# A two-layer diffusion backbone on one core: the layer norms' sums get precedence in the planned order, and constants and conditioning are prepared behind the first gated mixer

## The chip, the cores and the metric

The kernel runs on one core of one Trainium2 chip. The core has a matrix engine (TensorE, PE in the profile), three engines for elementwise work (VectorE: DVE, ScalarE: ACT, GpSimd: POOL) and a queue for transfers (SyncE: SP); each works through its own list of instructions in a fixed order and waits for the others by semaphores. The metric is device time in microseconds (us) of one execution; less is better.

## The reference

One inference step of a backbone with two layers, on 640 tokens (512 latent and 128 context) of 1024 channels. Each layer modulates its input by the conditioning (adaLN), runs three mixers side by side, merges them under gates, and ends both halves in a layer norm:

```python
def trunk_layer(x, cvec, l, P, pos, ctx):
    mod = jax.nn.silu(cvec) @ P['ada_w'][l] + P['ada_b'][l]
    sh1, sc1, g1, sh2, sc2, g2 = jnp.split(mod, 6, axis=-1)
    mix, ctx_out = token_mixer(x * (1.0 + sc1) + sh1, l, P, pos, ctx)
    x = layer_norm(ALPHA * x + g1 * mix, P['ln_g'][l, 0], P['ln_b'][l, 0])
    ff = conv_ffn(x * (1.0 + sc2) + sh2, l, P)
    x = layer_norm(ALPHA * x + g2 * ff, P['ln_g'][l, 1], P['ln_b'][l, 1])
    return x, ctx_out
```

`token_mixer` holds mixer A (retention, which needs the decays `log_sigmoid(ret_decay)`), mixer B (gated linear attention, the "gated mixer") and mixer C (differential attention, the third mixer, which needs one number lambda and a scaled gain per layer). There are four layer norms in all: mixer norm and FFN norm of the first layer, and the same of the second, whose FFN norm is the end of the program. Everything is computed in float32.

## The kernel before

**Tiles.** Activations lie transposed, as eight row tiles of 128 channels by 640 tokens. A projection streams its weights in blocks of 128 x 1024: SP loads `w`, ACT copies it to `whi` (a rounded high part), DVE or POOL subtracts to get `wlo`, and PE makes three matmuls of each piece: high weights by high input (`hh`), high by low input (`hl`), low weights by `hh`. Tokens come in two halves: the first is columns 256 to 640, in profile rows a 128x384 piece on PE and pieces of 256 and 128 on DVE and ACT; the second is columns 0 to 256.

**What sets the order.** The program is not issued as it is written. `Program.add` records every operation with its engine (some may go to DVE or POOL: `ANY`), an estimated cost and what it depends on; `Program.place` then plans the lists of all engines at once: of the operations that are ready, each engine takes the one with the smallest key. The key is the operation's place in the written program plus its argument `late`; a negative `late` gives precedence. An operation may be taken ahead of its place only within a window of the matrix work. On ACT the planner also counts the loads of function tables. What comes out is issued in that order, and on the chip an engine whose next instruction waits lets nothing behind it pass.

**A layer norm.** The projection in front of it (`pout` after the mixers, `pdn` after the FFN) makes its eight output blocks for the first half of the tokens, then for the second. `residual` adds each to the stream `xa` (DVE) and sums the blocks into `acc`. For the first half, `norm` makes the mean by a matmul with a matrix of ones (`pm<-acc`), subtracts it from the eight blocks, squares them on ACT, adds the squares up in a chain, and makes the variance by a matmul (`pv<-sq`); ACT turns it into `rs` by Ln and Exp, each behind a load of its function table. For the second half, `Shift` subtracts an early mean `mu` from half of the sums, and lets PE sum the squares (`pm<-sq`) and the blocks (`pm<-xa`); its `norm` puts a correction on that: a second `mu`, which is the square of the rest of the mean, `rs<-pm,mu` on DVE, Ln, Exp, and a last subtraction `xa<-xa,pm` from each block. `to_h` makes the next projection's input of each block: `hf` (DVE), `hh` (ACT), `hl` (DVE). The next projection is `pfa`/`pfb` after a mixer norm, `pq`/`pk` of the second layer's gated mixer after the first FFN norm; the last norm writes the output. `rescale` (POOL) brings `xa` to the scale of the next residual while the projection runs.

**The start.** `ada_first` makes the first layer's modulation by matmuls `pada` from loads `wada`; then the first projection runs, with its first weights still on their way. `pvv` is the projection of the gated mixer's values. At the start the program as written also prepares, for both layers, the decays `lg` (a series of tiny operations on 128 x 12), the third mixer's `nlam` and `gc`, the gated mixer's `gb`, and the conditioning `sB` (times its sigmoid, four steps of 128 x 512), from which later modulations are dot products on DVE.

Line 535 is every matmul, 556 an ACT operation, 568 a tensor-tensor operation, 582 one with a scalar and a tensor; the names tell them apart. After the change these are 536, 557, 569 and 583.

Of the kernel before, what the change touches and what calls it, by code (L numbers as in the profile page):

```python
# [138 lines left out]
RES = (0, 0)  # L139
RESC = 2  # L140
# [345 lines left out]
def hybrid_kernel(ctx, tc, io):  # L486
# [94 lines left out]
    def stt(out, a, s, b, op0, op1, eng=DVE):  # L581
        prog.add(eng, lambda e: ENG[e].scalar_tensor_tensor(out=real(out), in0=real(a), scalar=real(s), in1=real(b),  # L582
                                                            op0=op0, op1=op1), [out], [a, s, b], vcost(out.n, nptr(s)),
                 port=two(a, b))
# [50 lines left out]
    dma(sms[0], io["sm"][0])  # L635
# [5 lines left out]
    dma(cst[:, 0:128], io["cst"][:, 0:128])  # L641
# [22 lines left out]
    def ada_first(i):  # L664

        l = 0
        ps = mslot("pada")
        for k in range(KD):
            w = row("wada")
            dma(w[:, 0:512], io["adaW"][i, k])  # L670
            r = 32 * (k % 4)
            mm(ps[r:r + 32, 0:512], sc32[:, k, :], w[:, 0:512], start=(k < 4), stop=(k >= 4), free=r > 0)
        ev = row("ev")
        act(ev[:, 0:512], ps[:, 0:512])

# [128 lines left out]
    def norm(u, acc, half):  # L804
# [7 lines left out]
        for k in range(8):  # L812
            yield
            tt(u[k][:, c], u[k][:, c], pm[:, pc], SUB)
            p, q = q, row("sq")
            act(q[:, c], u[k][:, c], AF.Square)
            if k:
                tt(q[:, c], q[:, c], p[:, c], ADD, ANY)
# [5 lines left out]
    class Shift:  # L824
# [11 lines left out]
        def square(self, k):  # L836
            q = row("sq")
            act(q[:, self.c], self.u[k][:, self.c], AF.Square)
            mm(self.part(512), C("o1024"), q[:, self.c], start=(k == SECOND[0]), stop=(k == SECOND[7]))
# [17 lines left out]
        def norm(self):  # L857
            u, c, rs, dd = self.u, self.c, row("rs"), self.m
            act(dd[:, c], self.part(0), AF.Square)
            tt(rs[:, c], self.part(512), dd[:, c], SUB)  # L860
# [533 lines left out]

    lgs, lams = [], []
    for l in range(L):
        src = sms[l][:, SM["lgp"][0]:SM["lgp"][0] + 12]
        e = tiny([128, 12], "e")
        act(e, src, AF.Abs)
        act(e, e, AF.Exp, scale=-1.0)  # L1400
        den = tiny([128, 12], "den")
        ts(den, e, 2.0, ADD)
        recip(den, den)
        z = tiny([128, 12], "z")
        tt(z, e, den, MUL)
        z2 = tiny([128, 12], "z2")
        tt(z2, z, z, MUL)
        s = tiny([128, 12], "s")
        memset(s, 2.0 / 15, DVE)
        for n in (13, 11, 9, 7, 5, 3, 1):  # L1410
            tt(s, s, z2, MUL)
            ts(s, s, 2.0 / n, ADD)
        tt(s, s, z, MUL)
        lg = ctile([128, 12], f"lg{l}")
        ts(lg, src, 0.0, ALU.min)
        tt(lg, lg, s, SUB)
        nlg = ctile([128, 12], f"nlg{l}")
        ts(nlg, lg, -1.0, MUL)
        lgs.append((lg, nlg))
        dl = S(l, "dl").rearrange("p (a b d) -> p a b d", a=2, b=2)  # L1420
        pr = row("pr")[:, 0:128].rearrange("p (a d) -> p a d", a=2)
        tt(pr, dl[:, :, 0, :], dl[:, :, 1, :], MUL)
        sl = tiny([128, 2], "sl")
        reduce(sl, pr, ADD)
        act(sl, sl, AF.Exp)
        lam_init = 0.8 - 0.6 * math.exp(-0.3 * l)
        nlam = ctile([128, 1], f"nlam{l}")
        tt(nlam, sl[:, 1:2], sl[:, 0:1], SUB)
        ts(nlam, nlam, -lam_init, ADD)
        gc = ctile([128, 1], f"gc{l}")  # L1430
        ts(gc, S(l, "sg"), 1.0 - lam_init, MUL)
        gb = ctile([128, 1], f"gb{l}")
        ts(gb, S(l, "gg"), 0.0625, MUL)
        lams.append((nlam, gc, gb))

    for x in (sB[:, 0], sB[:, 1]):
        th = row("th")
        for c in (slice(0, 512), slice(512, 1024)):
            act(th[:, 0:512], x[:, c], AF.Tanh, scale=0.5)
            ts(th[:, 0:512], th[:, 0:512], 0.5, MUL, 0.5, ADD)  # L1440
            tt(x[:, c], x[:, c], th[:, 0:512], MUL)
    pending += [(0, i) for i in range(16, 48)] + [(1, i) for i in range(48)]

    for l in range(L):
# [3 lines left out]
        mix_b(l, ws, hs, yb, save if l else lambda: None)  # L1448
        mix_a(l, ws, hs, ya)
# [55 lines left out]
        def residual(ps, j, half, gt, acc=None):  # L1505
            for p0, p1, g in PIECES:
                if half[0] <= p0 < half[1]:
                    stt(u[j][:, p0:p1], ps[:, P0 + p0:P0 + p1], gt[:, 2 * j + g:2 * j + g + 1], u[j][:, p0:p1], MUL, ADD)
# [238 lines left out]
```

## Time and profile before

| | |
|---|---|
| median of 3 runs | 2523.47 us (2523.02 to 2524.02) |
| the profiled execution | 2525.73 us, of which its span is 2524.0 us |
| PE busy | 2458.0 us, 97% of the span |
| DVE busy | 1613.0 us, 64% |
| ACT busy | 1114.4 us, 44% |
| POOL busy | 513.5 us, 20% |
| share of the DMA engines, main queue | 30.9% |
| mean granted clock of PE | 0.99 of full |

Rows of a group or a timeline give start, duration, engine, line, operation, what it writes and reads (`out<-in`), shapes and a count of like instructions; in brackets stands the idle time ahead of it and what ended that. "PEclk" is the granted PE clock as a share of full speed. PE is the engine that is nearly always busy, so what a change can move is in the few stretches where it waits or runs at a lower clock.

### The profile page before, as it was taken

What the parts mean: (1) busy time and instruction counts of PE and PEld (TensorE: products, weight loads), DVE (VectorE), ACT (ScalarE), POOL (GpSimd) and SP (SyncE); (2) the same over time, 40 slices, a digit from 0 to 9 for tenths busy, and PEclk for the clock granted to TensorE, in tenths of its full rate; (3) what the DMA queues carried; (4) which work ended last, traced back from release to release, by engine and by line L of the source; (5) the groups of instructions that cost most, each with busy time, mean ns of one, the idle gap of its engine ahead of it and who ended that gap; (6) DMA issues with size and microseconds to landing.
All of it is one profiled execution on the core that took longest, in us unless ns stands there. A gap on an engine that the chain in (4) does not pass through costs nothing.

```text
span 2524.0 us, 41456 instructions
## 1 busy us (share of the span) xinstructions
PE 2458.0 (97%) x16762; PEld 2338.9 (93%) x16762; DVE 1613.0 (64%) x2898; ACT 1114.4 (44%) x1813; POOL 513.5 (20%) x387
## 2 busy tenths in 40 slices
PE   7999999999999999999989999999999999999997
PEld 4898989999998999999979989999999989999997
DVE  5758678667698955666867667675444664334346
ACT  3576665444425322313356666554444353122234
POOL 0434022002151600000346521111013331000001
PEclk9999999999999999999989999999999999999999
DMA  7213222342542333333423133322324322222222
GB/s 274 86 63 124 99 79 94 112 157 88 176 141 92 126 116 108 107 123 114 141 86 104 53 121 106 97 96 70 105 66 144 101 67 76 76 76 73 79 70 92
DMA packets 99551, 263.85 MB, mean 105 GB/s; under 512 B 11168, under 2 KB 17696, under 8 KB 99232
## 3 DMA queue, kind: packets, MB, share of 16 engines
q1 hardware_dynamic: 99360, 261.21, 30.9%
q8 instruction: 132, 2.16, 0.3%
q14 instruction: 59, 0.48, 0.1%
HBM read 243.34 MB, written 17.83 MB: 103 GB/s over the span
## 4 chain that ended last, share of the span: by engine, by line
PE 89%; DVE 6%; ACT 3%; issue 1%; DMA 1%; SPq 0%; ACTq 0%
PE pmm L535 13%; PE pfb L535 12%; PE pfa L535 12%; PE pdn L535 12%; PE pvv L535 7%; PE pbr L535 6%; PE pout L535 4%; PE pcq L535 2%; PE pck L535 2%; PE pag L535 2%; PE psc L544 2%; PE pr L535 2%; PE ptc L535 1%; PE psl L544 1%; PE paq L535 1%; PE po L535 1%
## 5 line engine op out<-in xcount | busy, mean ns | idle before, releaser
L556 ACT ACTIVATE whi<-w 128x1024 fp32r<-128x1024 f32 (+1 forms) x318 | 330.7, 1041 | 829.0 <-PE pdn L535 215.7
L568 DVE TENSOR_TENSOR wlo<-w,whi 128x1024 fp32r<-128x1024 f32 (+1 forms) x276 | 355.4, 1288 | 327.1 <-ACT whi L556 310.7
L568 POOL TENSOR_TENSOR wlo<-w,whi 128x1024 fp32r<-128x1024 f32 (+2 forms) x42 | 98.8, 2353 | 1192.8 <-ACT whi L556 991.2
L535 PE MATMUL pmm<-hh,whi 128*128 128x384 f32 (+1 forms) x768 | 241.3, 314 | 0.0
L535 PE MATMUL pmm<-hh,wlo 128*128 128x384 f32 (+1 forms) x768 | 241.0, 314 | 0.0
L535 PE MATMUL pmm<-hl,whi 128*128 128x384 f32 (+1 forms) x768 | 240.4, 313 | 0.0
L535 PE MATMUL pfa<-hl,whi 128*128 128x384 f32 (+1 forms) x704 | 219.0, 312 | 4.7 <-DVE hl L582 4.6
L535 PE MATMUL pfb<-hh,whi 128*128 128x384 f32 (+1 forms) x704 | 219.9, 312 | 0.0
L535 PE MATMUL pfa<-hh,whi 128*128 128x384 f32 (+1 forms) x704 | 218.8, 311 | 1.1 <-ACT hh L556 0.5
L535 PE MATMUL pfb<-hl,whi 128*128 128x384 f32 (+1 forms) x704 | 219.7, 312 | 0.0
L535 PE MATMUL pfb<-hh,wlo 128*128 128x256 f32 (+1 forms) x704 | 218.9, 311 | 0.4 <-DVE wlo L568 0.4
L535 PE MATMUL pdn<-fh,whi 128*128 128x384 f32 (+1 forms) x704 | 218.5, 311 | 0.0
L535 PE MATMUL pfa<-hh,wlo 128*128 128x384 f32 (+1 forms) x704 | 218.5, 310 | 0.0
L535 PE MATMUL pdn<-fl,whi 128*128 128x384 f32 (+1 forms) x704 | 218.2, 310 | 0.0
L535 PE MATMUL pdn<-fh,wlo 128*128 128x384 f32 (+1 forms) x704 | 217.8, 309 | 0.0
L535 PEld LDWEIGHTS pmm<-hh,whi 128*128 128x128 f32 x768 | 144.8, 189 | 3.7 <-issue 0.5
L535 PEld LDWEIGHTS pmm<-hh,wlo 128*128 128x128 f32 x768 | 144.8, 189 | 2.7 <-issue 1.1
L535 PEld LDWEIGHTS pmm<-hl,whi 128*128 128x128 f32 x768 | 144.6, 188 | 1.2 <-issue 0.5
L535 PE MATMUL pvv<-wlo,hh 128*128 128x256 f32 (+1 forms) x480 | 135.9, 285 | 4.1 <-DVE wlo L568 3.2
L535 PEld LDWEIGHTS pfa<-hl,whi 128*128 128x128 f32 x704 | 132.8, 189 | 6.9 <-DVE hl L582 6.9
L535 PE MATMUL pvv<-whi,hh 128*128 128x256 f32 (+1 forms) x480 | 137.4, 287 | 1.8 <-ACT q L556 1.0
L535 PE MATMUL pvv<-whi,hl 128*128 128x256 f32 (+1 forms) x480 | 136.9, 285 | 0.7 <-ACT z L556 0.7
(393 smaller groups left out, 6806.1 us busy)
## 6 DMA issues: line engine op xcount, KB each, us to landing
w<-W SPq DMA_DIRECT2D x270, 512.0 KB, 3.5
wada<-adaT SPq DMA_DIRECT2D x160, 256.0 KB, 3.9
w<-W SPq DMA_DIRECT2D x42, 448.0 KB, 3.2
gate<-g SPq DMA_DIRECT2D x32, 320.0 KB, 2.2
g<-gate SPq DMA_DIRECT2D x32, 320.0 KB, 4.8
wada<-adaW SPq DMA_DIRECT2D x32, 256.0 KB, 5.2
x<-xT SPq DMA_DIRECT2D x8, 320.0 KB, 6.1
dist<-rc SPq DMA_DIRECT2D x8, 320.0 KB, 4.9
```

Of the source, the lines that this page charges most:

```text
L535: prog.add(("PE",), lambda e: nc.tensor.matmul(real(out), real(lhsT), real(rhs), start=start, stop=stop), [out], [lhsT, rhs], {"PE": c})
L544: nc.tensor.matmul(real(o), real(w), real(r), start=start, stop=stop)
L556: prog.add(("ACT",), lambda e: nc.scalar.activation(out=real(out), in_=real(in_), func=func, **{k: real(x) for k, x in kw.items()}), [out] ...
L568: prog.add(eng, lambda e: ENG[e].tensor_tensor(out=real(out), in0=real(a), in1=real(b), op=op), [out], [a, b], vcost(out.n), late=late, po ...
```

## The change

Three things are changed, and no operation is added or taken away:

1. A constant `URGE = -300` is given as `late` to the sums of the layer norms: in `norm` the subtraction of the mean, the squares and their adds; in `Shift` the squares, the correction's square and `rs`; and the residual of the second half. Ln and Exp had it already.
2. The transfers of the first constants (`cst`, 128 columns) and of the first layer's small parameters (`sms[0]`) are issued behind the eight weight loads of the first modulation block instead of ahead of all.
3. The decays, `nlam`, `gc` and the steps on `sB` are put in a function `prepare()`, called after the first layer's gated mixer instead of ahead of it. `gb` stays.

```diff
+URGE = -300
...
-    def stt(out, a, s, b, op0, op1, eng=DVE):
+    def stt(out, a, s, b, op0, op1, eng=DVE, late=0):
...
-    dma(sms[0], io["sm"][0])
...
-    dma(cst[:, 0:128], io["cst"][:, 0:128])
...
+        if i == 0:
+            dma(cst[:, 0:128], io["cst"][:, 0:128])
+            dma(sms[0], io["sm"][0])
...
-            tt(u[k][:, c], u[k][:, c], pm[:, pc], SUB)
+            tt(u[k][:, c], u[k][:, c], pm[:, pc], SUB, late=URGE)
             p, q = q, row("sq")
-            act(q[:, c], u[k][:, c], AF.Square)
+            act(q[:, c], u[k][:, c], AF.Square, late=URGE)
             if k:
-                tt(q[:, c], q[:, c], p[:, c], ADD, ANY)
+                tt(q[:, c], q[:, c], p[:, c], ADD, ANY, late=URGE)
...
-            act(q[:, self.c], self.u[k][:, self.c], AF.Square)
+            act(q[:, self.c], self.u[k][:, self.c], AF.Square, late=URGE)
...
-            act(dd[:, c], self.part(0), AF.Square)
-            tt(rs[:, c], self.part(512), dd[:, c], SUB)
+            act(dd[:, c], self.part(0), AF.Square, late=URGE)
+            tt(rs[:, c], self.part(512), dd[:, c], SUB, late=URGE)
...
-    for x in (sB[:, 0], sB[:, 1]):
...
+    def prepare():
...
         mix_b(l, ws, hs, yb, save if l else lambda: None)
+        if l == 0:
+            prepare()
         mix_a(l, ws, hs, ya)
...
-                    stt(u[j][:, p0:p1], ps[:, P0 + p0:P0 + p1], gt[:, 2 * j + g:2 * j + g + 1], u[j][:, p0:p1], MUL, ADD)
+                    stt(u[j][:, p0:p1], ps[:, P0 + p0:P0 + p1], gt[:, 2 * j + g:2 * j + g + 1], u[j][:, p0:p1], MUL, ADD,
+                        late=URGE if acc is not None and half == HALF[1] else 0)
```

What it does to the order is seen at three places. On every engine the same instructions are issued as before, but for a few that go to the other of DVE and POOL: eight `wlo` from DVE to POOL, four adds of squares from POOL to DVE. In the long stretches between the places the order is as it was.

**The start, on DVE, ahead of the first `wlo` of `pvv`.** Here `s`, `z` belong to the decays, `th` and `sB` to the conditioning, `sl` and `wa` to the gated mixer. Before:

```order
L568 TENSOR_TENSOR wa<-wa_235,wa 32x512
L568 TENSOR_TENSOR s<-s,z_643 128x12
L576 TENSOR_SCALAR th<-th 128x512
L574 TENSOR_SCALAR s<-s 128x12
L568 TENSOR_TENSOR sB<-sB,th 128x512
L568 TENSOR_TENSOR s<-s,z_643 128x12
L568 TENSOR_TENSOR wlo<-w,whi 128x864
```

After:

```order
L569 TENSOR_TENSOR wa<-wa_231,wa 32x512 x2
L583 SCALAR_TENSOR_TENSOR hl<-hf,mod_71,hh 128x256
L569 TENSOR_TENSOR sl<-s_238,sq 64x512 x2
L569 TENSOR_TENSOR wlo<-w,whi 128x864
L569 TENSOR_TENSOR wlo<-w,whi 128x576
```

The decays and the conditioning are gone from there; they stand some fifty to a hundred and thirty rows further down, beside the second half of the gated mixer.

**The mixer norm of the first layer, on ACT** (the second layer's is alike). `rs<-rs` are Ln and Exp of the second half, each behind a table load. Before:

```order
L556 ACTIVATE hh<-hf,mb_103 128x128
L556 ACTIVATE hh<-hf,mb_103 128x256
L556 ACTIVATE hh<-hf,mb_103 128x128
L556 ACTIVATE sq<-xa 128x256
L556 ACTIVATE mu<-pm 128x256
L478 ACT_TABLE_LOAD
L556 ACTIVATE rs<-rs 128x256
L478 ACT_TABLE_LOAD
L556 ACTIVATE rs<-rs 128x256
L556 ACTIVATE hh<-hf,mb_103 128x256
```

After:

```order
L557 ACTIVATE sq<-xa 128x256 x4
L557 ACTIVATE hh<-hf,mb_103 128x256
L557 ACTIVATE sq<-xa 128x256
L557 ACTIVATE whi<-w 128x1024
L557 ACTIVATE mu<-pm 128x256
L557 ACTIVATE hh<-hf,mb_103 128x128
L557 ACTIVATE hh<-hf,mb_103 128x256
L479 ACT_TABLE_LOAD
L557 ACTIVATE rs<-rs 128x256
L479 ACT_TABLE_LOAD
L557 ACTIVATE rs<-rs 128x256
L557 ACTIVATE hh<-hf,mb_103 128x128
```

The correction of the second half now comes behind the first `hh` piece of the first block, where before five blocks of `hh` stood ahead of it. The other engines follow: on DVE `rs<-pm,mu` and five `xa<-xa,pm` stand ahead of the first `hl` of 128x128, and on PE all eight sums of squares stand ahead of the first `pfa`, where before seven did, and 24 `pout` stood between them and `pfa`; `pv<-sq` moved from behind the sixth of them to ahead of the first.

**The FFN norm of the first layer, on DVE.** Before:

```order
L582 SCALAR_TENSOR_TENSOR hf<-xa,ms_105,rs 128x128
L582 SCALAR_TENSOR_TENSOR hf<-xa,ms_105,rs 128x256
L582 SCALAR_TENSOR_TENSOR hf<-xa,ms_105,rs 128x128
L582 SCALAR_TENSOR_TENSOR hl<-hf,mb_106,hh 128x128
L582 SCALAR_TENSOR_TENSOR xa<-pdn,mod_71,xa 128x256
L568 TENSOR_TENSOR xa<-xa,pm 128x256 x2
L568 TENSOR_TENSOR rs<-pm,mu 128x256
L568 TENSOR_TENSOR xa<-xa,pm 128x256 x6
L582 SCALAR_TENSOR_TENSOR hl<-hf,mb_106,hh 128x256
```

After:

```order
L583 SCALAR_TENSOR_TENSOR hf<-xa,ms_105,rs 128x256
L569 TENSOR_TENSOR xa<-xa,mu 128x256 x2
L583 SCALAR_TENSOR_TENSOR xa<-pdn,mod_71,xa 128x256 x2
L569 TENSOR_TENSOR xa<-xa,mu 128x256 x2
L583 SCALAR_TENSOR_TENSOR xa<-pdn,mod_71,xa 128x256 x2
L569 TENSOR_TENSOR xa<-xa,mu 128x256 x4
L583 SCALAR_TENSOR_TENSOR hl<-hf,mb_106,hh 128x256
L583 SCALAR_TENSOR_TENSOR hf<-xa,ms_105,rs 128x128
```

The last residual (`xa<-pdn`) of the second half stood behind four blocks of `hf` and `hl`; now it stands ahead of the first `hl`, but the first `hf`, which needs the first half's `rs`, stands ahead of the early subtractions. And on ACT at the same place the early `mu` moved behind the first half's Ln and Exp; before, it stood ahead of the squares and both table loads. After:

```order
L479 ACT_TABLE_LOAD
L557 ACTIVATE rs<-pv 128x384
L557 ACTIVATE whi<-w 128x1024
L479 ACT_TABLE_LOAD
L557 ACTIVATE rs<-rs 128x384
L557 ACTIVATE mu<-pm 128x256
```

The last norm, at the end of the program, has the same two moves, and on ACT two `xa<-xa,sm` that stood between its last `mu` and the table load now stand ahead of that `mu`.

More of the change, by code (lines that the diff above doesn't have):

```diff
@@ L579, in ts @@
                  port=two(a, a))
-    def stt(out, a, s, b, op0, op1, eng=DVE):
+    def stt(out, a, s, b, op0, op1, eng=DVE, late=0):
         prog.add(eng, lambda e: ENG[e].scalar_tensor_tensor(out=real(out), in0=real(a), scalar=real(s), in1=real(b),
                                                             op0=op0, op1=op1), [out], [a, s, b], vcost(out.n, nptr(s)),
-                 port=two(a, b))
+                 port=two(a, b), late=late)
     def dot(out, a, b, acc):
@@ L1396, in hybrid_kernel @@
     for l in range(L):
[L1397 to L1431, printed above, removed]
         gb = ctile([128, 1], f"gb{l}")
         ts(gb, S(l, "gg"), 0.0625, MUL)
-        lams.append((nlam, gc, gb))
-    for x in (sB[:, 0], sB[:, 1]):
[L1437 to L1441, printed above, removed]
@@ L1442, in hybrid_kernel @@
-    pending += [(0, i) for i in range(16, 48)] + [(1, i) for i in range(48)]
+        lams.append([None, None, gb])
+    pending += [(0, i) for i in range(16, 48)] + [(1, i) for i in range(48)]
+    def prepare():
+        for l in range(L):
+            src = sms[l][:, SM["lgp"][0]:SM["lgp"][0] + 12]
+            e = tiny([128, 12], "e")
+            act(e, src, AF.Abs)
+            act(e, e, AF.Exp, scale=-1.0)
+            den = tiny([128, 12], "den")
+            ts(den, e, 2.0, ADD)
+            recip(den, den)
+            z = tiny([128, 12], "z")
+            tt(z, e, den, MUL)
+            z2 = tiny([128, 12], "z2")
+            tt(z2, z, z, MUL)
+            s = tiny([128, 12], "s")
+            memset(s, 2.0 / 15, DVE)
+            for n in (13, 11, 9, 7, 5, 3, 1):
+                tt(s, s, z2, MUL)
+                ts(s, s, 2.0 / n, ADD)
+            tt(s, s, z, MUL)
+            lg = ctile([128, 12], f"lg{l}")
+            ts(lg, src, 0.0, ALU.min)
+            tt(lg, lg, s, SUB)
+            nlg = ctile([128, 12], f"nlg{l}")
+            ts(nlg, lg, -1.0, MUL)
+            lgs.append((lg, nlg))
+            dl = S(l, "dl").rearrange("p (a b d) -> p a b d", a=2, b=2)
+            pr = row("pr")[:, 0:128].rearrange("p (a d) -> p a d", a=2)
+            tt(pr, dl[:, :, 0, :], dl[:, :, 1, :], MUL)
+            sl = tiny([128, 2], "sl")
+            reduce(sl, pr, ADD)
+            act(sl, sl, AF.Exp)
+            lam_init = 0.8 - 0.6 * math.exp(-0.3 * l)
+            nlam = ctile([128, 1], f"nlam{l}")
+            tt(nlam, sl[:, 1:2], sl[:, 0:1], SUB)
+            ts(nlam, nlam, -lam_init, ADD)
+            gc = ctile([128, 1], f"gc{l}")
+            ts(gc, S(l, "sg"), 1.0 - lam_init, MUL)
+            lams[l][0:2] = nlam, gc
+        for x in (sB[:, 0], sB[:, 1]):
+            th = row("th")
+            for c in (slice(0, 512), slice(512, 1024)):
+                act(th[:, 0:512], x[:, c], AF.Tanh, scale=0.5)
+                ts(th[:, 0:512], th[:, 0:512], 0.5, MUL, 0.5, ADD)
+                tt(x[:, c], x[:, c], th[:, 0:512], MUL)
```

## The prediction

> **What bounds the kernel now.** I read the page first: shares of the engines, the chain that ended last. Then the waits of PE, then its clock by stretches, and last the timeline of the stretches in which it waits.
>
> ```profile
> span 2524.0 us, 41456 instructions
> PE 2458.0 (97%) x16762; PEld 2338.9 (93%) x16762; DVE 1613.0 (64%) x2898; ACT 1114.4 (44%) x1813; POOL 513.5 (20%) x387
> PE 89%; DVE 6%; ACT 3%; issue 1%; DMA 1%; SPq 0%; ACTq 0%
> ```
>
> PE works 97% of the span, and the change takes no matmul away. All that can be won lies in the 66 us (2524.0 − 2458.0) without PE work and in stretches at a lower clock. The waits of PE, in us in total, times, longest:
>
> ```profile
> PE pq L535 <- DVE hl L582: 6.4, 5, 2.4
> PE pada L535 <- DVE s L568: 6.3, 1, 6.3
> PE pfa L535 <- DVE hl L582: 4.6, 4, 2.1
> PE pvv L535 <- DVE wlo L568: 3.2, 2, 2.2
> PE pm L535 <- ACT sq L556: 3.0, 2, 1.7
> ```
>
> The 6.3 us are the very first matmul's and stay. The others are what the change speaks of: `pq` and `pfa` wait for a normed input, `pm` for a square, `pvv` for its weights. By stretches (start and end, length, busy time of PE, PEld, DVE, ACT, POOL, then PEclk, DMA share, GB/s), the start, a stretch behind it, first mixer norm, the FFN behind it, first FFN norm, second mixer norm, end:
>
> ```profile
> 40.00:80.00 40.00, 34.36 (x226) 28.95 (x226) 25.04 (x79) 20.03 (x46) 2.49 (x3) 1.00 0.28 99
> 140.00:180.00 40.00, 40.00 (x284) 37.36 (x283) 17.81 (x22) 30.91 (x48) 8.09 (x6) 1.00 0.14 45
> 762.00:822.00 60.00, 54.12 (x349) 49.54 (x348) 51.63 (x116) 34.84 (x61) 8.34 (x4) 0.94 0.29 97
> 822.00:1240.00 418.00, 418.00 (x2821) 418.00 (x2822) 280.82 (x558) 115.48 (x131) 65.14 (x39) 1.00 0.36 120
> 1248.00:1306.00 58.00, 49.93 (x296) 44.31 (x295) 49.29 (x94) 33.66 (x60) 26.52 (x23) 0.88 0.21 70
> 2000.00:2060.00 60.00, 55.44 (x350) 50.80 (x349) 45.91 (x96) 35.40 (x62) 13.54 (x7) 0.91 0.22 71
> 2485.00:2524.00 39.00, 25.46 (x183) 23.48 (x181) 27.85 (x58) 26.57 (x47) 7.95 (x6) 0.86 0.27 92
> ```
>
> In the FFN PE has no gap in 418 us; there nothing can be won. The row also gives the price of a matmul: 418.00 over 2821 is 0.148, half of them with 384 columns and half with 256, so about 0.178 and 0.119. At the norms it is idle 5.9, 8.1 and 4.6 us, and its clock falls: if the lower state is half speed (an estimate, no row shows it alone), 0.94 of 60 us is 7.2 us at half (2 × 0.06 × 60), 0.88 of 58 us is 13.9, 0.91 of 60 us is 10.8.
>
> **The start.** What `pvv` waits for:
>
> ```profile
> 58.17 0.92 ACT L556 ACTIVATE whi<-w 128x864 fp32r<-128x864 f32 x1
> 62.31 0.69 DVE L568 TENSOR_TENSOR sB<-sB,th 128x512 f32<-128x512 f32 x1
> 63.00 1.05 DVE L568 TENSOR_TENSOR wlo<-w,whi 128x864 fp32r<-128x864 f32 x1
> 64.11 0.40 PE L535 MATMUL pvv<-wlo,hh 128*128 128x288 f32 x1 [2.23 <-DVE wlo L568]
> ```
>
> `whi` is there at 59.1, but DVE works through decays and conditioning until 63.0. With these moved, `wlo` can run at about 59.2 to 60.2, ahead of 61.88, when PE comes to it (64.11 − 2.23). The wait goes whole: −2.2. What is late next is `q`, which one more square on ACT may hold up by some tenths; I count 0. The two transfers set behind eight weight loads are small, and the bytes ahead of the first projection's weights stay the same: 0, between −0.9 and +0.5. The moved work lands where the rows above show 140 to 180: PE busy 40.00 of 40, DVE 17.81. That cover hides it (four steps on `sB` of 0.42 and 0.69, some sixty tiny ones of 0.17). The gated mixer's own DVE work slides together with it, by at most one operation of 0.7 at a time; I count +0.5, between 0 and +2. If the cover were gone, the whole would cost about 4 × 1.11 + 60 × 0.17 = 15.
>
> **The mixer norms.** Rows of the first, on PE, DVE, POOL and ACT:
>
> ```profile
> 782.06 2.00 PE L535 MATMUL pm<-sq,cst 128*128 128x256 f32 x8 [1.72 <-ACT sq L556]
> 788.83 1.14 DVE L582 SCALAR_TENSOR_TENSOR hf<-xa,ms,rs 128x256 f32<-128x256 f32 x3 [0.56 <-ACT rs L556]
> 790.99 3.10 DVE L582 SCALAR_TENSOR_TENSOR hf<-xa,ms,rs 128x128 f32<-128x128 f32 x3
> 795.73 1.00 DVE L582 SCALAR_TENSOR_TENSOR hf<-xa,ms,rs 128x128 f32<-128x128 f32 x3
> 791.58 2.36 POOL L568 TENSOR_TENSOR wlo<-w,whi 128x1024 fp32r<-128x1024 f32 x1 [10.30 <-ACT whi L556]
> 791.41 0.87 ACT L556 ACTIVATE hh<-hf,mb 128x128 fp32r<-128x128 f32 x2
> 794.40 0.44 PE L535 MATMUL pfa<-hl,whi 128*128 128x384 f32 x1 [2.06 <-DVE hl L582]
> 799.26 0.38 ACT L556 ACTIVATE mu<-pm 128x256 f32<-128x256 f32 x1 [1.43 <-PE pm L535]
> 802.20 0.42 ACT L556 ACTIVATE rs<-rs 128x256 f32<-128x256 f32 x1 [1.26 <-DVE rs L568]
> 802.64 1.28 ACT L478 ACT_TABLE_LOAD   x1
> ```
>
> Here PE waits 1.72 for the squares, 2.06 for `hl`, and about 1.6 in four shorter waits, 5.4 in all, out of 5.9 idle. In the new order the first square's sum has 14 `pout` more ahead of it and six others some 30 (1.7 and 3.5 us), so the 1.72 goes. But the first half's input now stands behind the second half's correction, and I follow that from the end of the last `pm<-sq`, t = 0. ACT does `mu` by about 0.6 (latency 0.2, 0.38) and the first `hh` of 128 by 0.95: PE waits 0.95. PE then has three matmuls with `hh` (0.53) and needs `hl`, for which DVE first does `rs` and five subtractions at 0.34 (the FFN norm's row of six below: 2.07) and then `hl`: 0.6 + 0.34 + 1.7 + 0.3 = 2.9, so PE waits from 1.5 to 2.9, 1.4 more. Six matmuls on, at 4.0, it needs the second block's `hh`, and ACT has two pieces of `hh`, a table load, Ln, a table load and Exp ahead of that: 0.6 + 0.7 + 1.28 + 0.42 + 1.28 + 0.42 + 0.4 = 5.1: 1.1 more. Behind that a block takes PE nine matmuls, 1.6, and DVE two operations of 0.38 and two of 0.29 to 0.33, about 1.34, so it stays ahead. The waits become 3.5 instead of 5.4: −1.8. Bounds: 0 to −4.5. The second mixer norm idles 4.6 instead of 5.9 by the table above; the same new waits give −0.8, between +1 and −3.5. Both keep their stretch at the lower clock in this sum.
>
> **The first FFN norm.** The same on DVE, which carries this stretch:
>
> ```profile
> 1270.36 1.14 DVE L582 SCALAR_TENSOR_TENSOR hf<-xa,ms,rs 128x256 f32<-128x256 f32 x3 [1.63 <-ACT rs L556]
> 1283.84 0.42 DVE L568 TENSOR_TENSOR xa<-xa,pm 128x256 f32<-128x256 f32 x1 [2.29 <-ACT mu L556]
> 1285.58 0.42 DVE L568 TENSOR_TENSOR xa<-xa,pm 128x256 f32<-128x256 f32 x1 [1.31 <-PE pm L535]
> 1286.25 2.07 DVE L568 TENSOR_TENSOR xa<-xa,pm 128x256 f32<-128x256 f32 x6
> 1297.53 2.67 DVE L582 SCALAR_TENSOR_TENSOR hf<-xa,ms,rs 128x256 f32<-128x256 f32 x3
> 1303.30 0.57 DVE L582 SCALAR_TENSOR_TENSOR hl<-hf,mb,hh 128x256 fp32r<-128x256 f32 x1 [0.58 <-ACT hh L556]
> ```
>
> `pq` and `pk` need only 6 × 0.178 = 1.07 of PE per block, less than DVE's 1.34, so PE follows DVE here until 1303.9, when the last `hl` is done. DVE idles 1.63 + 2.29 + 1.31 + 0.58 = 5.8 on the way, because the second half's sums begin only when four blocks of the first are out. In the new order they come before. Against that the early `mu` now waits behind `pv`, Ln and Exp: a table load, Ln, one `whi`, a table load and Exp are 1.28 + 0.49 + 0.9 + 1.28 + 0.53 = 4.5 behind `pv`, against 2.1 us of `pdn` that PE has in the meantime: PE waits about 2.5 there, for the first `pm<-xa`. Chaining DVE from there with the times above: first `hf` at 1265, the residuals out at about 1270, `pm` done at 1275, two blocks of `pq` and the first `pvv` meanwhile, correction and eight subtractions to 1281, then six blocks of the first half at 1.34 (8) and eight of the second at 0.76 (6): 1295. The rows at 1297.53 (2.67 for three, where 1.14 is usual) show what POOL's rescaling adds, here some 3 to 4 more: 1298.8 instead of 1303.9, so −5.1. Bounds: 0, if POOL adds as much as DVE's idle time took, and −8.
>
> **The end.**
>
> ```profile
> 2510.56 0.70 PE L535 MATMUL pm<-xa,cst 128*128 128x256 f32 x2 [1.36 <-DVE xa L582]
> 2512.14 1.11 ACT L556 ACTIVATE xa<-xa,sm 128x384 f32<-128x384 f32 x2
> 2513.26 1.28 ACT L478 ACT_TABLE_LOAD   x1
> ```
>
> The two `xa<-xa,sm` of 1.11 no longer stand between `mu` and the table load, on which Ln, Exp and the output wait: −1.0. PE's wait of 1.36 becomes one for the late `mu`, about 1.6: +0.2. Together −0.8, between +1 and −2.
>
> **The sum.** −2.2 + 0.5 − 1.8 − 0.8 − 5.1 − 0.8 = −10.2. The profiled execution took 2525.7, 1.7 outside its span; that becomes 2515.5. The median shown is 2.3 lower, so 2523.5 − 10.2 = 2513.3 there.
>
> **The rivals.**
>
> A, the lower clock goes too. If the spread-out waits (at most 1.4 at a time) no longer bring the clock down, the mixer norms win half of 7.2 and 10.8, 3.6 and 5.4, more: down to 2504; with one of them 2508. For it: in the stretch 40 to 80 a wait of 2.23 left the clock at 1.00. Against it: at the mixer norm a longest wait of 2.06 came with 0.94, and the new waits lie as close together. The Trainium skill, "TensorE: Matmul & The Clock Gate", Part 1, has the clock fall after an idle window of about 3.4 us; by it no wait of the new order would lower the clock and this rival would hold. The trace does not agree for the order before, where 2.06 was enough, so I trust the rule little.
>
> B, the gain is eaten by DVE and POOL. The change gives POOL eight `wlo` more. The row at 790.99 shows what one costs: three `hf` took 3.10 beside POOL's 2.36, the same three 1.00 without it (795.73), so 2.1. Were three or four of them to fall on the path at the norms, 6 to 8 us come back: 2519 to 2522. For it: planned times do not hold on the chip to a microsecond. Against it: while PE waits for a correction, DVE waits too, and a collision in that time costs nothing. The Trainium skill, "SBUF — State Buffer", Who interferes with whom, says a DVE instruction with two SBUF inputs and a GpSimd one that reads SBUF take turns whole; 790.99 agrees, and by that page the eight would cost up to 17.
>
> C, slower, by one mechanism: the second half's correction holds up the first half's input. It stands in front of it on DVE and ACT in fixed order, so whatever delays the last `pm<-sq` (a late residual, a square behind a `whi`) now delays `pfa` itself. My sum has 3.5 of waits per mixer norm; from 5.4 on the norm loses, and each further 10 us at half clock costs 5. Three norms at 5 each on top of the forecast make 2528.5, the point from which the kernel is slower; two collisions with POOL (4.2) and the clock (3.5) at each would give about 2536.
>
> D, the start does nothing, since another weight or `q` is late there at once: 2515.5, inside the forecast's own range of 2508 to 2518.
>
> **How the numbers follow.** The forecast with D 0.47, A 0.20, B 0.20, C 0.13. A difference of 0.2%, 5 us, is about what a measurement can tell here from none: faster is below 2518.4, slower above 2528.5. The forecast and A give faster, with little of B: 0.67; same 0.20; slower 0.13. The time is the forecast's, 2513. The range reaches down to A's 2503 and up to 2524, past B; left out are most of C and a little of A.
>
> **What would show it.** In the profile after: no `pvv` wait for `wlo` near 60 us; in the mixer norms no `pm` wait for `sq`, but waits of `pfa` for `hh` and `hl` of 1 to 1.5 each; at the FFN norm one wait of `pm` for `xa` of 2.5 and the last `hl` about 5 earlier; PEclk at the norms 0.88 to 0.94 as before. At 140 to 180 PE still 40 of 40. The prediction is wrong if `pfa` waits over 5 in a mixer norm, if the clock differs, or if POOL's `wlo` stand beside `hf`.

## The result, and the profile after

The changed kernel takes 2509.43 us (median of 4 runs, 2507.91 to 2512.82); the kernel before took 2523.66 us beside it (4 runs). The ratio is 0.9946, 95% interval 0.9929 to 0.9963: 14.2 us less. The forecast was 2513, its range 2503 to 2524. So the sign and the size were right; the reasons held only in part, and the size was right partly by luck, as shown below. The profiled execution of the changed kernel is its slowest of the four: 2512.82 us, of which the span is 2511.0, so the two traces stand 13.0 us apart.

The page of the changed kernel, the same lines as were shown of before (span and instructions, busy time, shares of the chain that ended last):

```profile
span 2511.0 us, 41475 instructions
PE 2449.1 (98%) x16762; PEld 2333.4 (93%) x16762; DVE 1616.1 (64%) x2895; ACT 1113.7 (44%) x1813; POOL 530.2 (21%) x390
PE 90%; DVE 6%; ACT 2%; issue 1%; DMA 1%; SPq 0%; ACTq 0%; DVEq 0%
```

PE has the same 16762 matmuls, yet it is busy 8.9 us less (2458.0 before), while the span shrank by 13.0. The same work in less busy time points to a higher clock: that is the first sign. Some of the waits of PE (us in total, times, longest):

```profile
PE pm L536 <- DVE xa L583: 6.6, 5, 2.9
PE pada L536 <- DMA wada<-adaW: 4.0, 1, 4.0
PE psl L545 <- DVE st L604: 3.5, 5, 1.9
PE pq L536 <- DVE hl L583: 3.5, 3, 2.1
PE pfa L536 <- ACT hh L557: 2.8, 4, 0.8
PE pfa L536 <- DVE hl L583: 2.6, 2, 1.3
PE pvv L536 <- DVE wlo L569: 1.2, 1, 1.2
```

`pq` for `hl` went from 6.4 to 3.5, `pfa` for `hl` from 4.6 to 2.6, `pvv` for `wlo` from 3.2 to 1.2. In their place stands a line that was not among those shown before: `pm` for `xa`, 6.6. By stretches, each as long as its counterpart in the prediction (start and end, length, busy time of PE, PEld, DVE, ACT, POOL, then PEclk, DMA share, GB/s): behind the start, first mixer norm, its FFN, first FFN norm, second mixer norm, end:

```profile
140.00:180.00 40.00, 40.00 (x285) 38.37 (x285) 27.05 (x73) 31.15 (x52) 11.05 (x8) 1.00 0.12 41
759.00:819.00 60.00, 53.85 (x362) 51.24 (x361) 48.53 (x108) 36.50 (x63) 20.97 (x9) 0.97 0.30 102
819.00:1237.00 418.00, 418.00 (x2824) 418.00 (x2823) 285.19 (x568) 113.24 (x129) 61.72 (x38) 1.00 0.36 121
1243.00:1301.00 58.00, 50.22 (x319) 43.93 (x318) 50.72 (x95) 34.59 (x62) 30.71 (x24) 0.97 0.22 72
1992.00:2052.00 60.00, 56.67 (x385) 53.91 (x385) 48.85 (x101) 40.11 (x67) 24.95 (x10) 0.97 0.27 88
2472.00:2511.00 39.00, 25.07 (x177) 22.68 (x175) 28.51 (x59) 26.22 (x47) 7.72 (x5) 0.88 0.27 92
```

Idle time of PE (length less busy) at the first mixer norm is 6.2 us where it was 5.9, at the FFN norm 7.8 for 8.1, at the second mixer norm 3.3 for 4.6. PEclk is 0.97 at all three, where it was 0.94, 0.88 and 0.91. In the same lengths PE got 362, 319 and 385 matmuls done instead of 349, 296 and 350.

To split the 13.0 us I took both traces between the same matmuls. Each matmul counts with what it takes in the gapless FFN (0.178 us for 384 columns, 0.119 for 256); what it takes more in a stretch at the lower clock is the second column (its price is in the rows of the next fence); what is left is time in which PE streams nothing. All in us, before to after:

| stage | whole | of it extra at the lower clock | of it without work |
|---|---|---|---|
| start, to 250 | 250.0 to 247.1: -2.9 | 2.4 to 2.9: +0.6 | first matmul -2.3, later -1.2 |
| first mixer norm and FFN | 478.1 to 475.6: -2.5 | 2.1 to 1.5: -0.6 | -1.9 |
| first FFN norm | 94.9 to 91.7: -3.1 | 4.1 to 1.5: -2.6 | -0.5 |
| second layer's gated mixer | 165.1 to 165.9: +0.8 | 0 | +0.8 |
| second mixer norm and FFN | 480.0 to 473.7: -6.3 | 3.2 to 1.1: -2.2 | -4.1 |
| end | 43.9 to 44.9: +1.0 | 0 | +1.0 |

The two long stretches between move by +0.2 and -0.1. So of the gain at the three inner norms, 11.9 us, some 5.4 is the clock and 6.5 time without work. This is an account of PE's time, not yet of causes: where PE follows another engine, a slow matmul may only fill time in which it would have waited. The first mixer norm after the change, on PE, shows the lower clock itself (start, duration, engine, line, operation, tiles, shapes, count; idle time ahead and what ended it):

```profile
779.67 0.67 PE L536 MATMUL pm<-xa,cst 128*128 128x256 f32 x2 [2.94 <-DVE xa L583]
...
790.46 0.44 PE L536 MATMUL pfa<-hh,whi 128*128 128x384 f32 x1 [0.76 <-ACT hh L557]
...
792.54 0.44 PE L536 MATMUL pfa<-hl,whi 128*128 128x384 f32 x1 [1.29 <-DVE hl L583]
...
794.60 0.44 PE L536 MATMUL pfa<-hh,whi 128*128 128x384 f32 x1 [0.75 <-ACT hh L557]
...
795.40 0.52 PE L536 MATMUL pfa<-hl,whi 128*128 128x384 f32 x1
795.72 0.52 PE L536 MATMUL pfa<-hh,wlo 128*128 128x384 f32 x1
...
799.05 0.34 PE L536 MATMUL pfa<-hl,whi 128*128 128x384 f32 x1
799.23 0.34 PE L536 MATMUL pfa<-hh,wlo 128*128 128x384 f32 x1
```

Matmuls of 384 columns start 0.32 us apart from 795.40 on and 0.18 apart from 799.05 on: the lower state gives a little over half of the rate, and each matmul caught in it costs 0.14 more, about 1.5 us in a full stretch of 3.41 us.

### The profile page after: what moved, and what is told of

It is laid out like the page before. It is cut to its first block, busy times and chain, and to the rows that moved or that the text cites. A ratio compares the mean times of both kernels' runs of the same rounds, so it can differ in the third digit from the quotient of the medians.

```text
span 2511.0 us, 41475 instructions
## 1 busy us (share of the span) xinstructions
PE 2449.1 (98%) x16762; PEld 2333.4 (93%) x16762; DVE 1616.1 (64%) x2895; ACT 1113.7 (44%) x1813; POOL 530.2 (21%) x390
## 4 chain that ended last, share of the span: by engine, by line
PE 90%; DVE 6%; ACT 2%; issue 1%; DMA 1%; SPq 0%; ACTq 0%; DVEq 0%
PE pmm L536 12%; PE pfb L536 12%; PE pfa L536 12%; PE pdn L536 12%; PE pvv L536 7%; PE pbr L536 5%; PE pout L536 4%; PE pcq L536 2%; PE pck L536 2%; PE pag L536 2%; PE pr L536 2%; PE psc L545 2%; PE ptc L536 1%; PE psl L545 1%; PE paq L536 1%
## 5 line engine op out<-in xcount | busy, mean ns | idle before, releaser
L569 DVE TENSOR_TENSOR wlo<-w,whi 128x1024 fp32r<-128x1024 f32 (+1 forms) x268 | 344.3, 1286 | 335.1 <-ACT whi L557 330.9
L569 POOL TENSOR_TENSOR wlo<-w,whi 128x1024 fp32r<-128x1024 f32 (+2 forms) x50 | 122.8, 2459 | 1186.2 <-ACT whi L557 987.4
L536 PEld LDWEIGHTS pfa<-hh,whi 128*128 128x128 f32 x704 | 132.9, 189 | 4.4 <-ACT hh L557 4.4
```

Source lines behind the costliest of these rows:

```text
L536: prog.add(("PE",), lambda e: nc.tensor.matmul(real(out), real(lhsT), real(rhs), start=start, stop=stop), [out], [lhsT, rhs], {"PE": c})
L569: prog.add(eng, lambda e: ENG[e].tensor_tensor(out=real(out), in0=real(a), in1=real(b), op=op), [out], [a, b], vcost(out.n), late=late, po ...
```

## The experiments

Two theories stood from here. Waits (W in the expectations): the new order gives PE less to wait for, as the prediction summed it. Clock (K where a text shortens it): it changes how the waits are spread, and with that how long PE runs at the lower clock behind them. Each run stands beside runs of before on the same chip, whose medians were 2524.64 to 2524.85 there.

**The parts.** `again` is the changed kernel once more, `sums_clean` is before with the precedence alone, `start_only` the start alone, `prepare_only` the start without the moved transfers:

```diff
# sums_clean: before, plus
+URGE = -300   (and each late=URGE of the change)
# start_only: the changed kernel
-URGE = -300
+URGE = 0
# prepare_only: start_only, with
+    dma(sms[0], io["sm"][0])
+    dma(cst[:, 0:128], io["cst"][:, 0:128])
...
-        if i == 0:
-            dma(cst[:, 0:128], io["cst"][:, 0:128])
-            dma(sms[0], io["sm"][0])
```

> The changed kernel once more, for its spread. Its four runs so far were 2507.9 to 2512.8 with granted clocks of 0.997 to 0.994, the kernel before 2523.0 to 2524.0. Theory K: the times again differ by up to 5 us, and the slower runs are those with the lower granted clock, about 1.7 us for each half-clock stretch of 3.4 us. Theory W: the spread is that of the kernel before, about 1 us, and does not follow the clock.

Measured: 2510.28 us (5 runs, 2509.37 to 2512.19), ratio 0.994, 0.9927 to 0.9954. The result repeats. Its spread of 2.8 us doesn't decide between the theories, since 23 runs of before on that chip spread over 3.7 (2522.79 to 2526.46); the fastest two of the five have a mean clock of 0.996 and the others 0.995.

> Moved transfers and moved preparation alone, no precedence. By the trace of the changed kernel PE is 2.75 us earlier at 245 us; so 2520.7. If the start gains only in company with the norms' order: within 1 us of 2523.5. The waits and the clock at the norms are as before.

Measured: 2521.42 (11 runs, 2517.93 to 2524.17), 0.9984, 0.9975 to 0.9993: 3.4 us.

> Moved preparation alone, transfers first as before. My prediction's step (the wait of 2.2 for the first wlo of pvv goes, the moved transfers are worth 0): same as start_only within 0.5 us. Rival (the transfers are worth the 1.2 us that PE was early at 15 to 47 us): 1.2 us slower than start_only, about 2522.

Measured: 2525.75 (11 runs, 2522.86 to 2526.40), 1.0002, 0.9993 to 1.0011: nothing. Its trace is 3.9 us ahead of before at 250 us, and 1.6 ahead of `start_only`, and loses most of that behind it; yet its median is 4.3 above that of `start_only`, whose profiled run was its slowest. Behind 260 us both have the order of before on every engine. At the norms the trace has 37.5 us at the lower clock, `start_only` 34.1 and before 30.7, and the mean clocks of its executions are 0.988 to 0.990, against 0.989 to 0.992. So the clock may be part of it; why it falls more here is not shown.

> The kernel before with the edits of precedence alone and its start left word for word (sums_only had rearranged the start too, and PE was 3.2 us later at 250 us there). If the two parts of the change add up: 2510.3 plus the start's 2.5 to 3, 2513. If the start's part is worth more in company: 2516 to 2517, which is sums_only less its 3.2.

Measured: 2514.95 (5 runs, 2514.77 to 2517.34), 0.9963, 0.995 to 0.9975: 9.8 us. With the 3.4 of `start_only` that makes 13.2 of the 14.6 that the whole change gave in `again`; the parts add up within their intervals.

Two runs were to be these parts and are not clean. In `sums_only` (precedence alone) and `transfers_only` (the two transfers alone) the preparation was written as a function called ahead of the first layer, which rearranged the start: `pvv` waits 4.63 us for `wlo` in `sums_only` where before waits 2.23.

> Precedence for the norms' sums alone; transfers and preparation as in the kernel before. If the two parts add up, it takes what the four norms gained in the two traces, about 2523.5 - 10 = 2513 to 2514. Theory W (the waits of PE shrank): the waits of PE in the three norms within the program sum to at least 5 us less than before, and the granted clock there is as before. Theory K (the clock): the waits sum to within 2 us of before's 17, and what is won is in the stretches at half clock, which shorten from about 24 us behind the mixer and FFN norms to about 10 (each 3.4 us less is 1.7 us won).

Measured: 2519.68 (7 runs, 2514.99 to 2520.61), 0.9974, 0.9963 to 0.9985. Its trace, from the fastest of the seven (2514.99), needs 3.2 us more than before up to 250 us and has no lower clock at either mixer norm. `sums_clean` replaced it.

> Moved transfers alone, preparation at its old place, no precedence. With both start parts 2521.4, with the preparation alone 2525.8, the kernel before 2524.9. If the transfers carry the start's gain on their own: 2520.5 to 2521.5. If they are worth 0, as I predicted, and the 4 us between the other two come from where waits fall in the clock's windows: 2524 to 2526. They could also be slower: the decays then wait for the parameters, which arrive at 10.5 us instead of 3.8, and stand ahead of the first wlo of pvv: 2527.

Measured: 2528.27 (11 runs, 2526.59 to 2528.76), 1.0014, 1.0005 to 1.0022: slower. Its trace needs 2.3 us more than before up to 250 us, and `pvv` waits 4.9 for `wlo`, close to the 4.63 of `sums_only`, so the rearranged start is the likely reason. What the transfers are worth alone can't be read from it.

**Which half's precedence.** The changed kernel, with `late=URGE` left only in `norm` (first half of the tokens), or only in `Shift` and the residual (second half):

```diff
# first_half_only
-            act(q[:, self.c], self.u[k][:, self.c], AF.Square, late=URGE)
+            act(q[:, self.c], self.u[k][:, self.c], AF.Square)
...
-            act(dd[:, c], self.part(0), AF.Square, late=URGE)
-            tt(rs[:, c], self.part(512), dd[:, c], SUB, late=URGE)
+            act(dd[:, c], self.part(0), AF.Square)
+            tt(rs[:, c], self.part(512), dd[:, c], SUB)
...
-                        late=URGE if acc is not None and half == HALF[1] else 0)
+                        late=0)
# second_half_only
-            tt(u[k][:, c], u[k][:, c], pm[:, pc], SUB, late=URGE)
+            tt(u[k][:, c], u[k][:, c], pm[:, pc], SUB)
...
-            act(q[:, c], u[k][:, c], AF.Square, late=URGE)
+            act(q[:, c], u[k][:, c], AF.Square)
...
-                tt(q[:, c], q[:, c], p[:, c], ADD, ANY, late=URGE)
+                tt(q[:, c], q[:, c], p[:, c], ADD, ANY)
```

> The changed kernel with precedence only for the first half's norm (subtraction, squares, adds), not for the second half's squares, correction and residual. The order then keeps the second half's correction behind the first half's input, as before. If the clock's fall at the norms comes from the long waits of pfa and pq for hl (2.06 and 2.41), which this order keeps: about 2520. If it is the early variance of the first half that wins: 2511.

Measured: 2524.18 (11 runs, 2522.67 to 2525.63), 1.0, 0.9991 to 1.0009. Neither forecast came. The run still has the moved start, which gave 3.4 in `start_only`; beside that run the precedence of the first half costs some 3 us (2.9 by the gains over before), near the edge of the intervals. Against `start_only` its trace wins 1.8 and 4.0 us at the two mixer norms with their FFNs and loses 3.8 at the first FFN norm and 2.8 at the end. Its FFN norm takes 98.3 us by the table's measure (94.9 before), since the second half's squares now come late. PE in that stretch:

```profile
1265.62 1.22 PE L536 MATMUL pm<-sq,cst 128*128 128x256 f32 x2 [2.87 <-ACT sq L557]
1268.10 2.93 PE L536 MATMUL pm<-sq,cst 128*128 128x256 f32 x6 [1.26 <-ACT sq L557]
...
1286.54 0.69 PE L536 MATMUL pq<-hh,whi 128*128 128x384 f32 x1 [2.35 <-ACT hh L557]
```

Its end takes 46.6 us (43.9 before).

> The other part: precedence only for the second half. The early mu stays ahead of the first half's Ln and Exp, and the correction stands ahead of the first half's input. If this carries the gain, 2509 to 2512, and the last norm does not lose the 1.0 that it lost in the changed kernel. If both are needed: 2516 to 2520.

Measured: 2512.82 (5 runs, 2510.47 to 2514.67), 0.9951, 0.9939 to 0.9964: 11.9 us of the 14.6 of `again`, with overlapping intervals. Without the start's 3.4, that is 8.5 of 11.1: the second half's sums and residual carry most of the gain of the precedence. Its end takes 45.2 us, so the loss there belongs to that half too.

**The clock by itself.** If it is the clock, filling PE's waits with throwaway matmuls should gain time without any reordering. `before_filled` is the kernel before, in its own order, with repeats of a matmul into unused columns of PSUM; `after_filled` the same in the changed kernel:

```diff
+    def mm_idle(out, lhsT, rhs, start, stop, n):
+        ...
+            for _ in range(n):
+                nc.tensor.matmul(real(o), real(lhsT), real(x), start=True, stop=True)
# before_filled
-            pq = project(ws, hs, "pq", "in", B_Q + 128 * t)
+            pq = project(ws, hs, "pq", "in", B_Q + 128 * t, fill={(256, 0, 1): 18, (256, 1, 1): 12, (256, 2, 1): 4} if l == 1 and t == 0 else {})
-                pa = project(ws, h2, "pfa", "up", f * 128)
+                pa = project(ws, h2, "pfa", "up", f * 128, fill={(256, 0, 1): 14} if f == 0 else {})
# after_filled
+            ... fill={(0, 3, 1): 26} if l == 1 and t == 0 else {})
+                ... fill={(256, 0, 0): 8, (256, 0, 1): 5} if f == 0 else {})
```

> The kernel before, order unchanged, with matmuls of 256 columns that repeat one of its inputs into unused columns and are thrown away, put where PE waits: 14 behind the first block of the first up projection in each layer (mixer norms; 1.65 us each in waits of 2.06) and 18, 12 and 4 behind the first three blocks of the second layer's q projection (FFN norm; waits of 2.41, 1.75 and 0.55). They add 62 x 0.12 = 7.3 us of PE work. Theory K (what costs at the norms is the clock that falls when PE idles): the stretches at half clock behind these waits go or shrink, and the kernel gets faster by 5 to 10 us although it does more, 2515 to 2520. Theory W (waits and work are what counts, the clock only follows): not faster, 2525 to 2528.

Measured: 2522.16 (11 runs, 2517.89 to 2523.11), 0.9987, 0.9978 to 0.9996: 2.5 us less, between the two forecasts. The throwaway matmuls, of 256 columns, are 14 in each mixer norm and 34 in the FFN norm. Its stretches, as for before (first mixer norm, first FFN norm, second mixer norm):

```profile
762.00:822.00 60.00, 55.41 (x359) 51.08 (x359) 51.68 (x116) 34.73 (x61) 8.38 (x4) 0.94 0.29 97
1248.00:1306.00 58.00, 52.05 (x343) 45.90 (x341) 50.29 (x94) 35.11 (x62) 28.25 (x24) 1.00 0.21 71
2000.00:2060.00 60.00, 56.29 (x365) 52.28 (x364) 46.73 (x98) 36.30 (x62) 15.10 (x8) 0.94 0.24 79
```

Only the FFN norm lost its lower clock (0.88 to 1.00); there the stage went from 94.9 to 93.0 us, although 34 matmuls of 0.119, 4.0 us, were added. The order there is that of before, and in the three other traces with that order at this norm (`start_only`, `prepare_only`, `transfers_only`) the stage takes 94.6 to 95.0. So the clock is worth at least 1.5 to 2 us at that norm; the change won 3.1 there. At the mixer norms the clock still fell, and little was won: there the clock's part rests on the table's account alone.

> The changed kernel with such matmuls in its own waits: in the mixer norms 8 behind the first matmul of the first up projection and 5 behind its first block (waits of 1.29 and 0.75), at the FFN norm 26 of 128 columns behind block four of the second half of q (wait of 2.10). Theory K: the half-clock stretches at 795, 1293 and 2024 go (1.7 us each), 2506 to 2508, and the runs lie within 2 us of each other. Theory W: 2510 to 2512, spread as before.

Measured (13 throwaway matmuls of 256 columns in each mixer norm, 26 of 128 in the FFN norm): 2510.70 (5 runs, 2507.95 to 2511.74), 0.9941, 0.9929 to 0.9954. Its stretches:

```profile
759.00:819.00 60.00, 55.38 (x386) 52.74 (x386) 49.87 (x111) 37.30 (x64) 21.84 (x9) 1.00 0.31 106
1243.00:1301.00 58.00, 51.99 (x350) 45.83 (x349) 49.56 (x93) 33.82 (x62) 31.52 (x25) 1.00 0.24 75
1992.00:2052.00 60.00, 57.96 (x408) 55.63 (x407) 49.97 (x102) 40.42 (x69) 24.99 (x10) 1.00 0.28 95
```

The clock is full at all three norms in the trace, yet the time is that of `again` (2510.28): it lies where the theory of waits had it, and both things that the theory of the clock forecast, the time and a spread within 2 us, failed. The throwaway matmuls' own 1.5 us a norm were covered by waits in the trace (the first mixer norm with its FFN 474.0 instead of 475.6, the second 472.7 instead of 473.7, but `again` has 472.7 there without them), but the medians show no gain. The mean clocks of its five executions, 0.995 to 0.997, are hardly above those of `again`, 0.995 to 0.996, so the run hardly changed what it was to test: it neither supports nor refutes a price of the clock.

**The early mean.** The prediction gave the late `mu` at the FFN norm a price of 2.5 us of waiting. `early_mu` puts it ahead of Ln and Exp again:

```diff
-                act(self.m[:, c], self.part(256), scale=2.0)
+                act(self.m[:, c], self.part(256), late=-1000, scale=2.0)
```

> The changed kernel with the early mu of the second half also given precedence (late = -1000), so that in the two FFN norms it no longer waits behind the first half's Ln and Exp. If the late mu costs what the trace shows, the wait of 1.62 at the FFN norm and of 0.69 and 0.58 at the end shrink: 2507 to 2508.5, and the last norm no longer loses the 1.0 it lost. Rival: DVE sets that stretch, the wait only moves: 2510 to 2511.

Measured: 2515.26 (5 runs, 2513.62 to 2519.54), 0.9963, 0.9951 to 0.9976: 5 us slower than the changed kernel. That is outside both forecasts. The order changed at the first FFN norm and in the second layer's gated mixer behind it; the last norm kept its order. The wait of `pm` for `xa` there shrinks from 1.62 to 0.52, and waits of `pq` for `hl` of 1.35 and 1.82 stand further on; the stage takes 93.5 us instead of 91.7. So the wait for `mu` did not set the end of that stage; what PE waits for last there is DVE's `hl`. The other 3 us are not placed by the trace.

**POOL beside DVE.** At the first mixer norm, the new wait of 2.94 on PE is for a residual that stands behind this on DVE:

```profile
774.00 5.13 DVE L569 TENSOR_TENSOR xa<-xa,mu 128x256 f32<-128x256 f32 x2
```

while POOL runs this:

```profile
772.66 6.19 POOL L569 TENSOR_TENSOR wlo<-w,whi 128x1024 fp32r<-128x1024 f32 x2 [3.07 <-ACT whi L557]
```

Two subtractions that take 0.76 elsewhere (at 1260.73) took 5.13 beside two `wlo` on POOL. `out_on_dve` is the changed kernel with the `wlo` of the `out` blocks, those of `pout`, put on DVE:

```diff
-            tt(lo[:, 0:n], w[:, 0:n], hi[:, 0:n].bitcast(F32), SUB, ANY)
+            tt(lo[:, 0:n], w[:, 0:n], hi[:, 0:n].bitcast(F32), SUB, DVE if blk[0] == "out" else ANY)
```

> The changed kernel with the wlo of the output projection's blocks kept on DVE (1.2 us each there) instead of DVE or POOL. Rival B's collision (two subtractions of mu took 5.13 beside POOL's wlo, where they take 0.76, and PE waited 2.94 for the block behind them) goes: 2508, if 2 us are won at the first mixer norm. In this order the early mu stands behind the first half's Ln and Exp in the mixer norms too; if that costs as much as at the FFN norm (1.6): 2510 to 2511.

Measured: 2512.61 (5 runs, 2511.86 to 2514.65), 0.9952, 0.994 to 0.9965: no gain. From 759 to 819 us PE idles 6.35 us, in the changed kernel 6.15: POOL now has other `wlo` there, and the collision only moves. DVE and POOL in that run:

```profile
780.60 4.75 DVE L569 TENSOR_TENSOR xa<-xa,mu 128x256 f32<-128x256 f32 x2
...
787.12 3.24 DVE L569 TENSOR_TENSOR xa<-xa,mu 128x256 f32<-128x256 f32 x3
```

```profile
780.13 4.94 POOL L569 TENSOR_TENSOR wlo<-w,whi 128x1024 fp32r<-128x1024 f32 x2 [13.16 <-PE pout L536]
787.22 2.52 POOL L569 TENSOR_TENSOR wlo<-w,whi 128x1024 fp32r<-128x1024 f32 x1 [2.15 <-ACT whi L557]
```

No version was clearly faster than the changed kernel. Taken together, both theories hold in part: the precedence of the second half brings most of the gain, the clock's share in it is shown by a run at the first FFN norm alone, and the rest of the split between clock and waits is the table's account.

## Why the prediction was right, and where it was not

**The step that failed: "Both keep their stretch at the lower clock in this sum."** They did not, nor did the FFN norm. PEclk rose to 0.97 at all three, and the table gives 5.4 us to that. Rival A was this case; it was set at 0.20 and priced by the mixer norms alone (3.6 and 5.4), while the largest part, 2.6 us, came at the FFN norm, where the prediction counted no clock at all. By the prediction's own signs ("if the clock differs") its mechanism failed here, though its time came out. Rival A came true in part: one stretch of 3.41 us was left at each norm in the trace.

**The start (-2.2 + 0.5).** Measured -2.9 in the trace and 3.4 in `start_only`. The wait of `pvv` at 64 us is gone, as forecast. "The 6.3 us are the very first matmul's and stay" was wrong: it waits 4.02, because the two small transfers no longer stand ahead of its loads (5.92 in `prepare_only`, where they do); of those 2.3 us only 1.0 reaches the first projection (its first matmul at 22.00 instead of 23.03). The cover of the moved work held: PE is 40.00 of 40 at 140 to 180 with DVE at 27.05 instead of 17.81.

**The mixer norms (-1.8 and -0.8).** No `pm` waits for `sq` there, and `pfa` waits 0.76, 1.29 and 0.75, where 0.95, 1.4 and 1.1 had been worked out: followed row by row, the new chain came out well. Left out was that a residual could come late: `pm` waits 2.94 for it at the first norm, the collision with POOL that rival B named at another place. Time without work fell by 1.9 and 4.1 with the FFN behind; the first is the term as summed. The second was mis-sized by 3.3 us. The new waits there (0.78, 0.76, 1.29, 0.49) add up to 3.3, close to the 3.5 worked out, where before had 4.4; that is 1.1 of the 4.1. Another 0.9 lies in the gapless FFN behind, and some 2 in gaps that no row shows as a wait; neither is explained. (By the terms shown, 5.4 less 0.95, 1.4 and 1.1 is 1.95, not 1.8; that changes nothing.)

**The first FFN norm (-5.1).** Measured -3.1. The last `hl` starts at 1295.29 instead of 1303.30; of those 8.0 us 5.2 came from earlier stages. The order did what was said: the wait of `pm` for the late `mu` is there, with 1.62 instead of 2.5. But time without work fell by 0.5 only, since PE has a new wait of 2.1 for `hl` near the end, where DVE's last `hf` and `hl` run slowly beside POOL's rescaling (2.95 us for three `hf` at 1288.50, 2.47 for three `hl` at 1291.37); the rest is the clock.

**The end (-0.8).** Measured +1.0, the wrong sign. The rows:

```profile
2489.83 0.67 PE L536 MATMUL pm<-xa,cst 128*128 128x256 f32 x2 [0.69 <-DVE xa L583]
...
2497.43 0.70 PE L536 MATMUL pm<-xa,cst 128*128 128x256 f32 x2 [0.58 <-DVE xa L583]
...
2498.81 0.67 PE L536 MATMUL pm<-sq,cst 128*128 128x256 f32 x2 [0.68 <-DVE xa L569]
```

```profile
2499.97 0.38 ACT L557 ACTIVATE mu<-pm 128x256 f32<-128x256 f32 x1 [1.42 <-DVE xa L569]
2500.37 1.28 ACT L479 ACT_TABLE_LOAD   x1
```

The table load follows `mu` at once, as said: 0.40 behind it instead of 1.40. But the last square's sum and `mu` itself now wait, 0.68 and 1.42, for subtractions of `xa<-xa,pm`, which now stand ahead of them and read the same `pm`. From the last `pm<-xa` to the table load it is 2.94 us instead of 2.70 (2510.56 to 2513.26). The other 0.8 is lost earlier, in part in waits of `pm` that the old order did not have (0.46 at 2486.18, 0.69 at 2489.83).

**Not in the sum:** the second layer's gated mixer, +0.8. Its order changed too, on every engine, which the part on the change doesn't say. Behind the FFN norm `psl` now waits 0.92 and 0.65 for DVE, where the old order left 0.2. The rivals C and D did not come: the kernel is faster, and the start is worth 3.4.

So it was partly luck that 10.2 was near 13 to 14, because terms offset each other: the clock (-5.4) and the second mixer norm (-3.3) were missed, the FFN norm's waits (4.6 too much) and the end (1.8) were counted too well.

## What to carry to other kernels

When PE waits in pieces, sum the idle time over short stretches and ask what it does to the clock, before asking which wait is longest: here more time went into slow matmuls behind the waits than a single wait cost. Precedence in a planned order pays for what the next stage waits for (the sums of the tokens that come last), and it can lose at places where the work that it displaces was the cover. Take such a change apart by halves and by places: one half of the precedence carried most of the gain, and the other alone won at the mixer norms what it lost elsewhere.

## What the runs showed of the hardware

The clock changes on a fixed grid of 3.41 us. In each trace every change of PEclk lies on one such grid (in before 3, 5, 230, 232, 371, 374, 378, 379, 592, 595 and 733 steps behind the first change), whose place against the start of the program differs from run to run. Windows of that grid in before:

```profile
793.10:796.52 3.42, 1.42 (x5) 0.77 (x5) 3.42 (x9) 1.32 (x4) 0.84 (x1) 1.00 0.40 108
796.52:799.93 3.41, 2.98 (x7) 2.08 (x7) 1.12 (x4) 1.85 (x5) 0.00 (x0) 0.50 0.53 202
```

In the changed kernel:

```profile
774.53:777.94 3.41, 2.21 (x19) 2.00 (x17) 3.41 (x2) 1.06 (x1) 3.41 (x2) 1.00 0.58 184
777.94:781.36 3.42, 1.69 (x7) 1.35 (x8) 2.98 (x6) 1.78 (x3) 0.91 (x1) 1.00 0.70 255
...
2020.39:2023.81 3.42, 1.69 (x8) 1.38 (x9) 3.29 (x10) 3.37 (x6) 0.74 (x1) 1.00 0.44 146
2023.81:2027.22 3.41, 2.92 (x10) 2.40 (x9) 2.63 (x9) 2.46 (x7) 0.00 (x0) 0.50 0.02 10
```

And in the same kernel's other run, `again`, at the same place:

```profile
2020.88:2024.29 3.41, 1.84 (x9) 1.48 (x9) 3.41 (x11) 3.36 (x5) 0.60 (x1) 1.00 0.52 144
2024.29:2027.71 3.42, 2.67 (x16) 2.40 (x15) 2.63 (x9) 2.47 (x7) 0.00 (x0) 1.00 0.03 12
```

What PE did in one window goes with the clock of the next. With PE busy 1.42 of 3.42 the next ran at 0.50. With 1.69 it did so too at 2020.39; in the other run of the same kernel the grid lay 0.49 us later and the waits 0.33, so 0.16 later against the same waits; PE was busy 1.84, and the clock stayed full. The second mixer norm with its FFN took 1.0 us less there (472.7 instead of 473.7). The length of a single wait does not decide: the longest, 2.94 us, lies over the two windows from 774.53, 1.20 and 1.73 us idle, and left the clock alone, while in before the window from 793.10, with 2.00 idle of which the wait of 2.06 gave only 1.30, brought it down. Busy time as shown is no exact measure either (1.69 at 777.94 stayed, 1.69 at 2020.39 fell); with each matmul counted only for its streaming time (an estimate from the spacing of matmuls at full clock), all 53 falls of the clock in the fourteen traces, the first and the last of each left aside, came behind windows without work for some 60% or more of their length, and the largest share that left it full was about two thirds. So even this measure leaves a stretch that it does not decide. The clock came back only behind windows with at most some 30% without work, and it stayed low behind some from 25% up.

The Trainium skill, "TensorE: Matmul & The Clock Gate", Part 1, tells of a window of 3413 ns that runs free of the program, with half rate after an idle window; the grid and the granted clock of 0.50 agree with these rows, but in the traces of before and after no window at the norms was wholly idle, and some 60% without work could be enough.

Four executions of the changed kernel had mean clocks of 0.994, 0.996, 0.997 and 0.997 and spans of 2511.0, 2508.9, 2506.3 and 2506.0 us: the more of it at the lower clock, the longer. The table above is made from the first of them, so in the others the clock's part of the gain is probably larger. That the place of the grid makes these differences fits the two traces above; it was not tried by itself.
